# Row-wise squared deviation: two loads from two queues become three loads in one

## The chip, the cores and the metric

The kernel runs on one core of a Trainium2 chip. The metric is the device time of one execution in microseconds (us). Before the change it is 85.28 us, the median of three runs (85.15, 85.28 and 85.28).

## The reference

`x` has 1024 rows of 4096 float32 numbers. From every row its mean is taken away, and the result is squared:

```python
mean = np.mean(x, axis=axis, keepdims=True)      # axis = -1
return ((x - mean) ** 2).astype(np.float32)
```

16.78 MB are read and 16.78 MB are written.

## The kernel before

SBUF has 128 partitions, so each partition handles 8 of the 1024 rows. The kernel splits them into two tiles of four rows per partition (`Q = 4`, `ntiles = 2`). In DRAM the tile index is outermost: tile 0 is the first 512 rows, and partition p holds four neighbouring rows of them, 64 KB in one piece; the next partition's piece begins 64 KB further on. Both tiles have buffers of their own, so no load ever waits for a buffer.

Lines 40 to 48 issue the loads. Row 0 of tile 0 (16 KB per partition, 2 MB in all) is issued from GpSimd (L44), the other three rows of that tile (6 MB) from SP (L45), and the whole of tile 1 (8 MB) from SP (L47). Each of these three transfers has a semaphore of its own, and an instruction that needs a row waits for the transfer that brings it.

Lines 50 to 68 go through the tiles and their rows in order. For each row, VectorE (DVE) sums it with the sign turned (L55, `reduce_sum` with `negate`), multiplies the sum by 1/4096 (L58), and ScalarE (ACT) computes `Square(x + neg_mean)` in place (L59). After every second row (`H = 2`), SP issues a store of these two rows (L68, 4 MB). There are four stores, all in SP's queue.

The statements name what is computed; the order of the instructions on each engine is set by the framework's scheduler. On VectorE it is: reduce 0, mean 0, reduces 1 and 2, mean 1, reduce 3, means 2 and 3, reduces 4 and 5, mean 4, reduce 6, mean 5, reduce 7, means 6 and 7. A mean therefore often comes one reduce later than its own sum. SP issues its instructions in order: both loads, then the four stores, each after waiting for ACT's second row of the pair.

Of the kernel before, what the change touches and what calls it, by code (L numbers as in the profile page):

```python
# [2 lines left out]

os.environ.setdefault("NEURON_RT_ULTRASERVER_MODE", "4")

# [4 lines left out]

F32 = mybir.dt.float32


@with_exitstack
def kernel(
    ctx: ExitStack,
    tc: tile.TileContext,
    x: bass.AP,
    axis: bass.AP,
    out: bass.AP,  # L20
):


    nc = tc.nc

    B, D = x.shape
    P = nc.NUM_PARTITIONS
    Q = 4
    H = 2
    assert B % (P * Q) == 0  # L30
    ntiles = B // (P * Q)
    inv_d = 1.0 / float(D)

    x_t = x.rearrange("(n p q) d -> n p (q d)", p=P, q=Q)
    out_t = out.rearrange("(n p q) d -> n p (q d)", p=P, q=Q)

    io = ctx.enter_context(tc.tile_pool(name="io", bufs=ntiles))
    stats = ctx.enter_context(tc.tile_pool(name="stats", bufs=2 * ntiles * Q))

    tiles = []  # L40
    for i in range(ntiles):
        x_tile = io.tile([P, Q * D], F32)
        if i == 0:
            nc.gpsimd.dma_start(out=x_tile[:, :D], in_=x_t[i][:, :D])  # L44
            nc.sync.dma_start(out=x_tile[:, D:], in_=x_t[i][:, D:])  # L45
        else:
            nc.sync.dma_start(out=x_tile, in_=x_t[i])  # L47
        tiles.append(x_tile)

    for i in range(ntiles):  # L50
        for q in range(Q):
            row = tiles[i][:, q * D:(q + 1) * D]
            neg_sum = stats.tile([P, 1], F32)
            neg_mean = stats.tile([P, 1], F32)
            nc.vector.reduce_sum(  # L55
                out=neg_sum, in_=row, axis=mybir.AxisListType.X, negate=True
            )
            nc.vector.tensor_scalar_mul(out=neg_mean, in0=neg_sum, scalar1=inv_d)  # L58
            nc.scalar.activation(  # L59
                out=row,  # L60
                in_=row,
                func=mybir.ActivationFunctionType.Square,
                bias=neg_mean,
                scale=1.0,
            )
            if q % H == H - 1:
                part = slice((q + 1 - H) * D, (q + 1) * D)
                nc.sync.dma_start(out=out_t[i][:, part], in_=tiles[i][:, part])  # L68


# [1 line left out]
_INS = ['x', 'axis']  # L72
_OUTS = [((1024, 4096), 'float32')]

_NUMBERS = {'axis': -1}


# [26 lines left out]
```

## Time and profile before

| what | value |
|---|---|
| median of the three runs | 85.28 us |
| time of the profiled execution | 85.28 us |
| its span (first to last instruction) | 83.5 us |
| VectorE busy | 35.4 us in 16 instructions; a reduce takes 4.41 us |
| ScalarE busy | 30.7 us in 9 instructions; a row takes 3.70 us |
| bytes over the span | 33.55 MB, mean 402 GB/s |
| load of 6 MB, from issue (0.74) to landing | 21.5 us |
| load of row 0 by GpSimd, from issue (1.22) to landing | 24.0 us |
| load of 8 MB, from issue (1.17) to landing | 41.0 us |
| a store of 4 MB, from issue to landing | 11.2 to 14.7 us |

Transfers are cut into packets, which here are the pieces of one partition: 16, 48 or 64 KB for the loads and 32 KB for the stores. Sixteen DMA engines move them, eight partitions each. In the view by stretches of time, the two DMA columns count a packet wholly in the stretch in which it begins: a stretch shorter than a packet can show a share far above 1 or 0, and only the sums over a round of sixteen packets say how long a packet lasted. In the timeline, an instruction of SP's queue (SPq) is only the issue of a transfer; the transfer itself runs on for many microseconds.

### The profile page before, as it was taken

The page shows a single profiled execution, that of the slowest core. Times are in us where ns is not written, and L with a number is a line of the kernel's source. Part 1 is how long each engine was busy: PE and PEld are TensorE (multiplying, and loading weights), DVE is VectorE, ACT ScalarE, POOL GpSimd, SP SyncE. Part 2 cuts the span into 40 slices and gives each one's busy share as a digit, 9 for nine tenths or more (in the row PEclk, how much of TensorE's full clock was granted, in tenths as well). Part 3 has the DMA queues.
Part 4 walks back from the last instruction along what each step waited for, and adds up shares of the span by engine and source line. Part 5 has one row for each costly group of instructions (what it writes and reads, how often), then busy time and mean ns, then how long its engine had stood idle before and what let it go on. Part 6 is the DMA issues. An engine that isn't in the chain of part 4 may idle for free.

```text
span 83.5 us, 82 instructions
## 1 busy us (share of the span) xinstructions
DVE 35.4 (42%) x16; ACT 30.7 (37%) x9; POOL 0.8 (1%) x5
## 2 busy tenths in 40 slices
DVE  0000000000008999999999999999900000000000
ACT  0000000000006069105969992969799950000000
POOL 4000000000000000000000000000000000000000
DMA  9299999977999659999059599979959996995990
GB/s 306 94 424 439 494 502 502 432 330 330 667 502 471 282 251 502 502 502 502 0 251 502 251 502 502 439 314 502 502 251 502 502 471 282 502 502 251 502 502 0
DMA packets 1008, 33.55 MB, mean 402 GB/s; under 512 B 112, under 2 KB 112, under 8 KB 112
## 3 DMA queue, kind: packets, MB, share of 16 engines
q1 hardware_dynamic: 864, 31.46, 88.2%
q0 software_dynamic: 144, 2.10, 5.9%
HBM read 16.78 MB, written 16.78 MB: 402 GB/s over the span
## 4 chain that ended last, share of the span: by engine, by line
DVE 42%; DMA 29%; ACT 4%; ACTq 4%; issue 1%; POOLq 0%
DVE neg_sum L55 42%; DMA x_tile<-in_x_dram 29%; ACT x_tile L59 4%; ACTq L99 4%; DVE neg_mean L58 1%; POOLq L99 0%; POOLq L85 0%
## 5 line engine op out<-in xcount | busy, mean ns | idle before, releaser
L55 DVE TENSOR_REDUCE neg_sum<-x_tile 128x1 f32<-128x4096 f32 x8 | 35.0, 4410 | 25.3 <-DMA x_tile<-in_x_dram 25.3
L59 ACT ACTIVATE x_tile<-x_tile,neg_mean 128x4096 f32<-128x4096 f32 x8 | 29.4, 3704 | 11.9 <-DVE neg_mean L58 11.9
L59 ACT ACT_TABLE_LOAD x1 | 1.3, 1283 | 25.3 <-DMA x_tile<-in_x_dram 25.3
L58 DVE TENSOR_SCALAR neg_mean<-neg_sum 128x1 f32<-128x1 f32 x8 | 1.1, 148 | 0.0
L44 POOL DMA_DIRECT2D x_tile<-in_x_dram x1 | 0.7, 652 | 0.8 <-PEq L99 0.8
L85 POOL MEMSET const-bfloat16-1.0<- 128x1 bf16 x1 | 0.1, 96 | 0.0
L85 POOL MEMSET const-float32-0.0<- 128x1 f32 x1 | 0.1, 93 | 0.2 <-issue 0.2
L85 POOL MEMSET const-float32-1.0<- 128x1 f32 x1 | 0.1, 93 | 0.0
L85 POOL MEMSET const-uint8-127<- 128x1 uint8 x1 | 0.1, 93 | 0.0
## 6 DMA issues: line engine op xcount, KB each, us to landing
out_dram<-x_tile SPq DMA_DIRECT2D x4, 4096.0 KB, 13.0
x_tile<-in_x_dram SPq DMA_DIRECT2D x1, 6144.0 KB, 21.5
x_tile<-in_x_dram POOLq DMA_DIRECT2D x1, 2048.0 KB, 24.0
x_tile<-in_x_dram SPq DMA_DIRECT2D x1, 41.0
```

What stands on the lines that cost most here:

```text
L44: nc.gpsimd.dma_start(out=x_tile[:, :D], in_=x_t[i][:, :D])
L55: nc.vector.reduce_sum(out=neg_sum, in_=row, axis=mybir.AxisListType.X, negate=True)
L58: nc.vector.tensor_scalar_mul(out=neg_mean, in0=neg_sum, scalar1=inv_d)
L59: nc.scalar.activation(out=row, in_=row, func=mybir.ActivationFunctionType.Square, bias=neg_mean, scale=1.0,)
L85: nc = _bacc.Bacc("TRN2", target_bir_lowering=False, num_devices=1)
L99: with _tile.TileContext(nc) as tc:
```

## The change

The rows are assigned to partitions in another way: partition p now holds the 8 neighbouring rows 8p to 8p + 7 (128 KB in one piece), and the next partition's piece begins 128 KB further on. They are loaded in three transfers of two, four and two rows per partition (4, 8 and 4 MB; packets of 32, 64 and 32 KB), each into a buffer of its own, all issued from SP (L44 of the new file). GpSimd issues no transfer any more. The computation per row is the same, and after every second row a store of two rows (4 MB) is issued from SP (L64), so that there are again four. The diff, without the lines that only lose an indentation:

```diff
-    Q = 4
-    H = 2
-    assert B % (P * Q) == 0
-    ntiles = B // (P * Q)
+    R = B // P
+    LOADS = [2, 4, 2]
+    S = 2
+    assert B == P * R and sum(LOADS) == R
...
-    x_t = x.rearrange("(n p q) d -> n p (q d)", p=P, q=Q)
-    out_t = out.rearrange("(n p q) d -> n p (q d)", p=P, q=Q)
+    x_v = x.rearrange("(p r) d -> p (r d)", p=P)
+    out_v = out.rearrange("(p r) d -> p (r d)", p=P)
...
-    for i in range(ntiles):
-        x_tile = io.tile([P, Q * D], F32)
-        if i == 0:
-            nc.gpsimd.dma_start(out=x_tile[:, :D], in_=x_t[i][:, :D])
-            nc.sync.dma_start(out=x_tile[:, D:], in_=x_t[i][:, D:])
-        else:
-            nc.sync.dma_start(out=x_tile, in_=x_t[i])
-        tiles.append(x_tile)
+    for i, n in enumerate(LOADS):
+        x_tile = io.tile([P, n * D], F32, tag=f"x{i}")
+        nc.sync.dma_start(out=x_tile, in_=x_v[:, r0 * D:(r0 + n) * D])
+        rows += [(x_tile, k) for k in range(n)]
+        r0 += n
...
-            if q % H == H - 1:
-                part = slice((q + 1 - H) * D, (q + 1) * D)
-                nc.sync.dma_start(out=out_t[i][:, part], in_=tiles[i][:, part])
+        if r % S == S - 1:
+            nc.sync.dma_start(
+                out=out_v[:, (r + 1 - S) * D:(r + 1) * D],
+                in_=x_tile[:, (k + 1 - S) * D:(k + 1) * D],
+            )
```

In the changed kernel's order of instructions, VectorE runs reduces 0 and 1, means 0 and 1, reduces 2 and 3, mean 2, reduce 4, mean 3, reduce 5, mean 4, reduce 6, mean 5, reduce 7, means 6 and 7. Reduce 2 waits for the second transfer and reduce 6 for the third. SP issues three loads and then four stores.

More of the change, by code (lines that the diff above doesn't have):

```diff
@@ L27 @@
     P = nc.NUM_PARTITIONS
-    Q = 4
-    H = 2
-    assert B % (P * Q) == 0
-    ntiles = B // (P * Q)
+    R = B // P
+    LOADS = [2, 4, 2]
+    S = 2
+    assert B == P * R and sum(LOADS) == R
     inv_d = 1.0 / float(D)
-    x_t = x.rearrange("(n p q) d -> n p (q d)", p=P, q=Q)
-    out_t = out.rearrange("(n p q) d -> n p (q d)", p=P, q=Q)
-    io = ctx.enter_context(tc.tile_pool(name="io", bufs=ntiles))
-    stats = ctx.enter_context(tc.tile_pool(name="stats", bufs=2 * ntiles * Q))
-    tiles = []
@@ L41 @@
-    for i in range(ntiles):
-        x_tile = io.tile([P, Q * D], F32)
-        if i == 0:
-            nc.gpsimd.dma_start(out=x_tile[:, :D], in_=x_t[i][:, :D])
-            nc.sync.dma_start(out=x_tile[:, D:], in_=x_t[i][:, D:])
-        else:
-            nc.sync.dma_start(out=x_tile, in_=x_t[i])
-        tiles.append(x_tile)
[L50 to L56, printed above, removed]
-            )
[L58 to L65, printed above, removed]
-            if q % H == H - 1:
-                part = slice((q + 1 - H) * D, (q + 1) * D)
-                nc.sync.dma_start(out=out_t[i][:, part], in_=tiles[i][:, part])
+    x_v = x.rearrange("(p r) d -> p (r d)", p=P)
@@ new lines @@
+    out_v = out.rearrange("(p r) d -> p (r d)", p=P)
+    io = ctx.enter_context(tc.tile_pool(name="io", bufs=1))
+    stats = ctx.enter_context(tc.tile_pool(name="stats", bufs=2 * R))
+    rows = []
+    r0 = 0
+    for i, n in enumerate(LOADS):
[3 more added lines that the diff above has]
+        r0 += n
+    for r, (x_tile, k) in enumerate(rows):
+        row = x_tile[:, k * D:(k + 1) * D]
+        neg_sum = stats.tile([P, 1], F32)
+        neg_mean = stats.tile([P, 1], F32)
+        nc.vector.reduce_sum(
+            out=neg_sum, in_=row, axis=mybir.AxisListType.X, negate=True
+        )
+        nc.vector.tensor_scalar_mul(out=neg_mean, in0=neg_sum, scalar1=inv_d)
+        nc.scalar.activation(
+            out=row,
+            in_=row,
+            func=mybir.ActivationFunctionType.Square,
+            bias=neg_mean,
+            scale=1.0,
+        )
+        if r % S == S - 1:
+            nc.sync.dma_start(
+                out=out_v[:, (r + 1 - S) * D:(r + 1) * D],
+                in_=x_tile[:, (k + 1 - S) * D:(k + 1) * D],
+            )
```

## The prediction

> **What bounds the kernel now.** I read the page's DMA digits first, then the queues, then the chain, because the kernel moves 33.55 MB and computes little.
>
> ```profile
> DVE 35.4 (42%) x16; ACT 30.7 (37%) x9; POOL 0.8 (1%) x5
> ...
> DMA  9299999977999659999059599979959996995990
> ...
> q1 hardware_dynamic: 864, 31.46, 88.2%
> q0 software_dynamic: 144, 2.10, 5.9%
> ...
> DVE 42%; DMA 29%; ACT 4%; ACTq 4%; issue 1%; POOLq 0%
> ```
>
> The two queues' packets fill 88.2 + 5.9 = 94.1% of the 16 DMA engines' span: 78.6 of 83.5 us. Only 4.9 us of an average DMA engine is idle. The chain says something else (DVE 42%), and here it misleads: it covers 80% of the span and breaks off at ACT's last row, and the stores that fill the rest are not on it. DVE is busy for 35.4 us and ACT for 30.7 us. So the question is where the 4.9 us lie. The page's 40 slices blur this, because a packet is counted in the slice in which it begins (shares go over 1). I therefore took the stretches view around the places where a stage starts or ends; its last two columns are the DMA share and GB/s.
>
> ```profile
> 1.50:2.00 0.50, 0.00 (x0) 0.00 (x0) 0.38 (x1) 1.00 4.12 1278
> 2.00:2.50 0.50, 0.00 (x0) 0.00 (x0) 0.00 (x0) 1.00 0.60 197
> 2.50:3.00 0.50, 0.00 (x0) 0.00 (x0) 0.00 (x0) 1.00 0.27 98
> 4.00:4.50 0.50, 0.00 (x0) 0.00 (x0) 0.00 (x0) 1.00 2.27 983
> 4.50:5.00 0.50, 0.00 (x0) 0.00 (x0) 0.00 (x0) 1.00 1.36 590
> 38.50:39.00 0.50, 0.50 (x3) 0.38 (x1) 0.00 (x0) 1.00 3.32 1442
> 39.00:39.30 0.30, 0.30 (x1) 0.30 (x1) 0.00 (x0) 1.00 2.02 874
> 39.30:39.40 0.10, 0.10 (x1) 0.10 (x1) 0.00 (x0) 1.00 1.51 655
> 39.40:43.00 3.60, 3.60 (x3) 2.93 (x1) 0.00 (x0) 1.00 0.00 0
> 43.00:43.50 0.50, 0.50 (x2) 0.49 (x1) 0.00 (x0) 1.00 2.44 1049
> 44.00:44.50 0.50, 0.50 (x1) 0.50 (x1) 0.00 (x0) 1.00 1.72 721
> 44.50:45.00 0.50, 0.50 (x1) 0.50 (x1) 0.00 (x0) 1.00 0.78 328
> ```
>
> Two columns give the packets. In 43.0 to 43.5, 1049 GB/s x 0.5 us is 524 KB: 16 packets of 32 KB, one per DMA engine, and 2.44 x 0.5 us says 1.22 us each. In the same way the last round of loads (38.5 to 39.4) is 16 packets of 64 KB at (3.32 x 0.5 + 2.02 x 0.3 + 1.51 x 0.1) = 2.42 us; the second round (4.0 to 5.0) is 16 packets of 48 KB at 1.815 us; the first round takes (4.12 + 0.60 + 0.27) x 0.5 = 2.50 us for the same size, so starting cold costs 0.68 us. All warm sizes run near 27 KB/us per DMA engine: size hardly matters, so the engines' own rate is the limit.
>
> Now the hole. The last round of loads begins at 38.5 to 39.4 and lasts 2.42 us, so loading ends between 40.9 on the first DMA engine and 41.75 on the last (one packet begins alone in 39.3 to 39.4). No store packet begins before 43.0; a finer look puts all 16 between 43.2 and 43.4. Eleven of the 16 last load packets (1442 GB/s x 0.5 us) begin before 39.0, so the average engine ends near 41.3. **The DMA engines stand empty for 1.5 us on the latest and some 1.9 us on average.** The timeline says why:
>
> ```profile
> 25.27 4.42 DVE L55 TENSOR_REDUCE neg_sum<-x_tile 128x1 f32<-128x4096 f32 x1 [25.27 <-DMA x_tile<-in_x_dram]
> ...
> 38.62 3.71 ACT L59 ACTIVATE x_tile<-x_tile,neg_mean 128x4096 f32<-128x4096 f32 x1 [5.00 <-DVE neg_mean L58]
> 42.36 0.35 SPq L68 DMA_DIRECT2D out_dram<-x_tile  x1
> ```
>
> Row 0 is known to have landed only at 25.27, three reduces of 4.41 us follow before the mean of row 1 (issue order: reduce 0, reduces 1 and 2, mean 1), ACT ends row 1 at 42.33, SP issues the first store at 42.36, and its packets begin 0.9 us later. The other idle time is the start (packets from about 1.75) and the close (last store packets begin by 81.1, end by 82.3).
>
> **The change, part by part.**
>
> *Loads.* Bytes are equal. Per DMA engine, now: 8 packets of 48 KB, 8 of 16 KB (GpSimd's, 0.61 us), 8 of 64 KB: 8 x (1.815 + 0.61 + 2.42) + 0.68 = 39.4 us. After: 16 of 32 KB and 8 of 64 KB. A load packet of 32 KB is not in the trace; between twice the 16 KB packet (1.22) and two thirds of the 48 KB one (1.21) it is 1.21, so 16 x 1.21 + 8 x 2.42 + 0.68 = 39.4 us. Difference 0, at most 0.2 either way. The cold excess may be fixed (0.68) or go with size (0.45): at best -0.2.
>
> *GpSimd's issue* (0.65 us) and its queue go; the first packets come from SP's issue at 0.74 in both, so nothing at the start. A gain of 8 x 0.006 = 0.05 us is the upper bound from packets, and no loss is seen since no other instruction waits in POOL. *SP's third load* costs 0.4 us of issue (0.38 and 0.43 now) at 1.6, while the first load's packets run; SP's next work is the store at 29.5. Should SP be held until an earlier load drains, it is 12 us, still free.
>
> *Compute moves forward.* Load 0 (8 rounds) ends at about 1.75 + 0.75 of stagger + 0.68 + 8 x 1.21 = 12.9 on the latest DMA engine and is seen 0.3 to 0.4 later, as now (41.75 against 1.17 + 41.0 = 42.2): 13.2. The new issue order is reduce 0, reduce 1, both means; 13.2 + 2 x 4.4 + 0.1 = 22.1, and ACT's rows 0 and 1 end 2 x 3.7 later: **store 0 is issued at 29.5 instead of 42.36.** It must be there by 40.9: 11.4 us of cover, less 0.9 to the first packet.
>
> *Later stores.* Load 1 ends 8 x 2.42 = 19.4 later, seen at 32.5. The order lags by one: reduces 2, 3, mean 2, reduce 4, mean 3; mean 3 comes at 32.5 + 3 x 4.42 = 45.8, ACT row 3 ends at 49.6, store 1's packets are there at 50.5. Store 0 lasts from 40.9 (41.75 on the latest DMA engine) for 8 x 1.22 = 9.8, to 50.7 (51.5). The margin is 0.2 on the earliest and **1.0 us on the one that sets the end**: the thinnest cover in the plan. Store 2 is issued at about 58.4 for 60.5 (earliest engine), store 3 at 66.6 for 70.2. If load 1 were seen 2 us late, 1.0 us of the gain would go.
>
> *Sum.* The latest DMA engine ends its loads at 41.75 as now, then runs 32 x 1.22 = 39.04 without a hole: 80.8. Now the last packets end at 82.3. That is -1.5 us; landing and close (1.2 us) stay. Span 83.5 - 1.5 = 82.0. The profiled execution took 85.28, 1.78 beyond its span, and 85.28 is also the median: **83.8 us**. An average DMA engine gains 1.9, but the stagger that the first round leaves (0.75) is today swallowed by the hole and will now last to the end; that is why I take 1.5.
>
> *Row pitch.* Each partition's rows now lie 128 KB apart in DRAM instead of 64 KB. All packets of this trace have the old pitch, so the cost is bounded by its best and worst warm rows: stores at the loads' rate (1.21 for 1.22, -0.3 on 32) and every packet slowed like the second round of stores ((1.72 + 0.78) x 0.5 = 1.25 for 1.22: 2.5% of 78.5, +2.0). I take 0: warm packets of four sizes agree to about 1%.
>
> A rule speaks against this. The Trainium skill, "DMA: Bandwidth & Descriptors", section "Latency and other measured facts", lists copies that slow with a large power-of-two distance between partitions' rows: 207 GB/s at 512 KiB against 214 at full rate. If that 3% held here, an estimate from that page adds 2.6 us and makes 86.4; it has no figure at 128 KiB, and no row here shows a second pitch.
>
> Another advises loads and stores on different issuing engines: "Perfetto Trace Analysis", section "DMA Optimizations". By it, store 0 would not stand behind the loads from 29.5 to 41; as the DMA engines are full throughout, the sum stays the same.
>
> **Rivals.**
> 1. *The stagger goes too*, through a shorter first round or less spread at the start: the full 1.9 us is gained, 83.3. For: the stores' starts lie within 0.2 us. Against: the last loads still show the first round's spread 36 us later.
> 2. *Late stores*: store 1 misses its slot and half to all of the hole comes back there, 84.3 to 85.1. For: the margin of 0.2 to 1.0 us. Against: reduces last 4.41 us without scatter.
> 3. *It does not do what it says*: SP cannot queue a store behind unfinished loads, or the packets do not follow without a hole: 85.2. Against: the second load was issued at 1.17 behind 6 MB and followed without a hole.
> 4. *Slower*: the new pitch lengthens packets. It decides from 1.5 / 78.5 = 1.9%; at the bound of 2.5% it gives 85.28 - 1.5 + 2.0 = 85.8. For: it touches all 33.55 MB. Against: warm packets are equally fast at every size, so DRAM seems not to be the limit.
>
> **How the numbers follow.** Forecast 83.8: 0.64. Rival 1: 0.20. Rival 2: 0.08. Rival 3: 0.03. Rival 4: 0.05. The range takes in rival 1 with 0.2 us of packet gains (83.1) and half of rival 2 (84.7). About 0.2% (0.17 us) is what a measurement can tell: faster 0.92, same 0.03, slower 0.05.
>
> **What would show it.** No stretch without packet starts longer than a packet between 1.75 and 81; first store issued near 29.5, the next near 49.6, 58.4 and 66.6; the first reduce near 13.2; last landing near 81.2. A hole near 41 or 51, or warm packets above 1.22 us per 32 KB, would make the prediction wrong.

## The result and the profile after

The changed kernel takes 84.41 us (median of four runs, 84.27 to 84.47), the kernel before beside it 85.22 us (85.04 to 85.28). The ratio is 0.9906, with a 95% interval of 0.9885 to 0.9928: faster by 0.8 us. Forecast were 83.8 us and a gain of 1.5 us, so the sign was right and the time lies in the range, but only about half of the gain came. The profiled execution took 84.35 us with a span of 82.6 us.

From the page of the changed kernel, its queues and its chain:

```profile
DMA  8698990999999099799879998997998999799790
...
q1 hardware_dynamic: 1008, 33.55, 96.1%
...
DMA 37%; DVE 32%; ACT 4%; ACTq 4%; SPq 0%; issue 0%
```

The one queue now fills 96.1% of the DMA engines' span, 79.4 us of 82.6; before, two queues filled 94.1%, 78.6 us. So idle time fell from 4.9 to 3.2 us, but **the same bytes took 0.8 us more packet time**. That second number is what the forecast did not have. The chain again ends with ACT and says nothing about the stores.

The timeline confirms that compute moved forward as planned:

```profile
12.80 8.75 DVE L52 TENSOR_REDUCE neg_sum<-x_tile 128x1 f32<-128x4096 f32 x2 [12.80 <-DMA x_tile<-in_x_dram]
...
28.97 37.23 SPq L64 DMA_DIRECT2D out_dram<-x_tile  x4
```

The first reduce starts at 12.80 (before: 25.27) and store 0 is issued at 28.97 (before: 42.36), long before the loads end. Now the stretches around the places that the prediction spoke of; the last two columns are again DMA share and GB/s, and share times length is the mean duration of a packet if the stretch holds one round of sixteen:

```profile
1.50:2.50 1.00, 0.00 (x0) 0.00 (x0) 0.00 (x0) 1.00 1.78 492
2.50:3.50 1.00, 0.00 (x0) 0.00 (x0) 0.00 (x0) 1.00 0.08 33
37.40:38.00 0.60, 0.60 (x1) 0.00 (x0) 0.00 (x0) 1.00 2.02 874
38.50:39.50 1.00, 1.00 (x1) 0.00 (x0) 0.00 (x0) 1.00 1.72 524
39.50:40.00 0.50, 0.50 (x1) 0.00 (x0) 0.00 (x0) 1.00 0.00 0
40.00:41.00 1.00, 1.00 (x3) 0.02 (x1) 0.00 (x0) 1.00 1.76 524
41.00:41.90 0.90, 0.90 (x1) 0.90 (x1) 0.00 (x0) 1.00 0.00 0
41.90:42.80 0.90, 0.90 (x1) 0.90 (x1) 0.00 (x0) 1.00 1.36 583
79.30:80.30 1.00, 0.00 (x0) 0.00 (x0) 0.00 (x0) 1.00 1.21 524
```

524 GB/s over 1 us is 16 packets of 32 KB. The load round at 37.4 takes 2.02 x 0.6 = 1.21 us, as estimated for a warm load packet of this size. **The last two load rounds take 1.72 and 1.76 us.** The first round of stores (41.9) is back at 1.36 x 0.9 = 1.22, the last (79.3) is at 1.21. There is no hole: 39.5 to 40.0 and 41.0 to 41.9 are empty of starts only because packets last longer. So just ahead of the place where the 1.9 us hole was, two rounds of loads lose 0.51 + 0.55 = 1.06 us on the average DMA engine.

### The profile page after: what moved, and what is told of

It is laid out like the page before. It is cut to its first block, busy times and chain, and to the rows that moved or that the text cites. A ratio compares the mean times of both kernels' runs of the same rounds, so it can differ in the third digit from the quotient of the medians.

```text
span 82.6 us, 83 instructions
## 1 busy us (share of the span) xinstructions
DVE 35.4 (43%) x16; ACT 30.7 (37%) x9; POOL 0.2 (0%) x4
## 3 DMA queue, kind: packets, MB, share of 16 engines
q1 hardware_dynamic: 1008, 33.55, 96.1%
## 4 chain that ended last, share of the span: by engine, by line
DMA 37%; DVE 32%; ACT 4%; ACTq 4%; SPq 0%; issue 0%
DMA x_tile<-in_x_dram 37%; DVE neg_sum L52 32%; ACT x_tile L56 4%; ACTq L98 4%; SPq L44 0%; DVE neg_mean L55 0%
## 5 line engine op out<-in xcount | busy, mean ns | idle before, releaser
L56 ACT ACT_TABLE_LOAD x1 | 1.3, 1283 | 12.8 <-DMA x_tile<-in_x_dram 12.8
```

What stands on the lines that cost most here:

```text
L56: nc.scalar.activation(out=row, in_=row, func=mybir.ActivationFunctionType.Square, bias=neg_mean, scale=1.0,)
```

## The experiments

Three theories were on record before the first run. **Theory A**, the turn: load packets are stretched when stores stand in the queue behind them. **Theory B**: the addresses of the last rows, at the new row pitch, are slow to read. **Theory C**: something that runs between 38 and 43 us disturbs the loads. All times are medians; each ratio is to the kernel before, run on the same chip (85.05 to 85.14 us). All edits but one are made to the changed kernel.

### Store 0 held back by three passes of ACT

`PAD` is 3, and `pad` is a scratch tile of 128 x 4096 ones, so that row 1 is scaled by 1 but waits for the passes:

```diff
+        if r == 1:
+            nc.vector.tensor_scalar(
+                out=pad[:, 0:1], in0=neg_mean, scalar1=0.0, scalar2=1.0,
+                op0=mybir.AluOpType.mult, op1=mybir.AluOpType.add,
+            )
+            for _ in range(PAD):
+                nc.scalar.activation(
+                    out=pad, in_=pad, func=mybir.ActivationFunctionType.Square
+                )
...
-            scale=1.0,
+            scale=pad[:, 0:1] if r == 1 else 1.0,
```

> The changed kernel with three extra passes of ACT over a scratch tile ahead of row 1 (11 us, no other output changes), so that store 0 is issued near 40.0 and its packets come to the DMA engines near 40.9, when at most one load packet is left on each. Theory A: at most the last load packet is stretched, the gain over the changed kernel is 0.5 to 0.9 us: 83.5 to 83.9. Theories B and C: the same two rounds are stretched, 84.4 or more.

Measured: 83.46 us, ratio 0.982 (0.9805 to 0.9834), 1.0 us faster than the changed kernel although ACT does 11 us more, and slightly below the range given. Its stores in the timeline, and its stretches from the same load rounds on:

```profile
39.97 26.20 SPq L77 DMA_DIRECT2D out_dram<-x_tile  x4
...
38.40:39.40 1.00, 1.00 (x1) 1.00 (x1) 0.00 (x0) 1.00 1.21 524
39.40:40.60 1.20, 1.20 (x1) 0.55 (x1) 0.00 (x0) 1.00 1.01 437
40.60:41.10 0.50, 0.50 (x3) 0.14 (x1) 0.00 (x0) 1.00 0.00 0
41.10:42.00 0.90, 0.90 (x1) 0.90 (x1) 0.00 (x0) 1.00 1.36 583
42.00:43.20 1.20, 1.20 (x1) 1.20 (x1) 0.00 (x0) 1.00 1.04 437
```

The last two load rounds take 1.21 us each: same addresses, same time of day, no stretch, because store 0 was issued at 39.97 instead of 28.97. Theory B falls. Theory C falls as far as reduces go (VectorE is busy throughout in both). The second round of stores takes 1.04 x 1.2 = 1.25 us, a small thing that returns below.

### Held back by two passes, and by two and a half

The same edit with `PAD = 2`, and with passes of 4096, 4096 and 2048 columns.

> As the run with three extra passes of ACT, with two: store 0 is issued near 36.3 and is there near 37.2, four us before the loads end. Theory A: the stretch belongs to the last 64 KB (2.4 us), so four us ahead cost as much as twelve: 84.4. If the cost grows with the time that the store stands ready: about a third of it, 83.8.

> As the runs with two and with three extra passes of ACT, with two and a half: store 0 is issued near 38.2 and is there near 39.1, when about two load packets of 32 KB (1.8 to 2.5 us) are left on each DMA engine. Theory A, with the stretch bound to the time that a store stands behind the last 64 KB: between the two, 83.7 to 84.2. If the price is all or nothing: 84.4 or 83.4.

Measured: 84.38 us, ratio 0.9918 (0.9896 to 0.994), with two passes; 83.94 us, ratio 0.9867 (0.985 to 0.9883), with two and a half. With two:

```profile
36.35 29.82 SPq L77 DMA_DIRECT2D out_dram<-x_tile  x4
...
38.50:39.50 1.00, 1.00 (x1) 0.00 (x0) 0.00 (x0) 1.00 2.18 524
40.50:41.50 1.00, 1.00 (x3) 0.54 (x1) 0.00 (x0) 1.00 1.42 524
```

Store 0 is issued at 36.35 and the last two load rounds take 2.18 and 1.42 us: together 1.18 us too much, the full price. The runs with two and a half scatter from 83.92 to 84.34, and the profiled one was the 84.34; its rounds, 1.85 x 1.1 = 2.04 and 0.96 x 1.3 = 1.25 us, show 0.86 us of it. So four us ahead costs as much as twelve, and at about two us ahead (issued at 38.37) the times suggest that the price is paid in some executions and not, or not wholly, in others; only the slowest of the five has a trace.

### Stores with no link to the rows

```diff
-                in_=x_tile[:, (k + 1 - S) * D:(k + 1) * D],
+                in_=con,
```

> The four stores send a constant tile (filled by GpSimd at the start) instead of the squares, so that they wait for no row and stand in SP's queue from the first microseconds on; loads, reduces and squares run as in the changed kernel, but the squares are not stored. Theory A (the turn inside one queue costs by itself): the same two rounds of load packets, the last 64 KB of each DMA engine before the stores, are stretched to about 1.75 us, 84.4. Rival (the cost comes from storing rows that were only just computed, or from what computes at that time): no stretch, 83.4.

Measured: 84.5 us, ratio 0.9928 (0.9911 to 0.9944).

```profile
7.68 1.84 SPq L67 DMA_DIRECT2D out_dram<-con  x4
...
38.40:39.40 1.00, 1.00 (x1) 0.00 (x0) 0.00 (x0) 1.00 1.78 524
40.30:41.20 0.90, 0.90 (x3) 0.21 (x1) 0.00 (x0) 1.00 1.97 583
```

All four stores are issued by 9.5 us, and the last two load rounds still take 1.78 us each (1.78 x 1.0 and 1.97 x 0.9). The stretch starts after 38.4 as in the changed kernel, not when the stores were queued. What is stored, and what computes it, does not matter.

### How the price counts: packets of 64, 16 and 32 KB at the turn

First `LOADS = [2, 2, 4]`, so that the last load packet on each DMA engine is 64 KB; then the last load issued as two of one row, with 16 KB packets:

```diff
-        nc.sync.dma_start(out=x_tile, in_=x_v[:, r0 * D:(r0 + n) * D])
+        step = 1 if i == 2 else n
+        for j in range(0, n, step):
+            nc.sync.dma_start(
+                out=x_tile[:, j * D:(j + step) * D],
+                in_=x_v[:, (r0 + j) * D:(r0 + j + step) * D],
+            )
```

> Loads of two, two and four rows: the packets ahead of the queued stores are 64 KB instead of 32 KB, store 0 stands in the queue from about 29. Theory A, counted in bytes (the last 64 KB of each DMA engine): the one last load packet is stretched by about 1.1 us, from 2.42 to 3.5, 84.4. Counted in packets (the last two): both are stretched by some 45%, 85.5. If the price hangs on small packets: no stretch, 83.3.

> The changed kernel with its last load cut into two loads of one row (packets of 16 KB instead of 32 KB). Theory A, if the turn costs by bytes (the last 64 KB of each DMA engine): the last four packets are stretched, 84.4 as the changed kernel. Theory A, if it costs by packets (the last two): half, 83.9. Theories B and C: 84.4.

Measured: 84.41 us, ratio 0.9924 (0.9909 to 0.9938), and 84.41 us, ratio 0.9927 (0.9913 to 0.9942). Both equal the changed kernel. In the first, one round of 64 KB earlier and the last one (1049 GB/s x 1.0 us and 1311 x 0.8 are 16 packets each):

```profile
36.00:37.00 1.00, 0.00 (x0) 1.00 (x1) 0.00 (x0) 1.00 2.42 1049
38.40:39.20 0.80, 0.00 (x0) 0.25 (x1) 0.00 (x0) 1.00 4.58 1311
```

The last packet takes 4.58 x 0.8 = 3.66 us instead of 2.42: 1.24 us more, on one packet. In the kernel with 16 KB packets, the round begun at 38.6 takes 1.48 x 0.6 = 0.89 us and the next 1.94 x 0.6 = 1.16 us instead of 0.61, the third 1.46 x 0.7 = 1.02, and the fourth is normal again: 1.24 us in all. The price is thus 1.1 to 1.25 us whatever the packets, and it falls on about the last 64 KB of loads of each DMA engine. During it VectorE is idle in the 64 KB kernel and ACT nearly so, which removes theory C for good.

### Smaller stores behind the loads

`S = 1`: eight stores of one row.

> The changed kernel with eight stores of one row (16 KB packets) in place of four of two. Theory A with a price set by the loads' last 64 KB: the same two rounds of load packets are stretched, by 1.1 us in all, 84.4 to 84.6. If the price goes with the size of the store packets that stand behind the loads: half, 83.9.

Measured: 84.73 us, ratio 0.9958 (0.9943 to 0.9972). That is 0.1 us above the range given. The last two load rounds take 1.64 and 0.99 x 2.0 = 1.98 us, 1.2 us too much in all. The price does not fall with the size of the store packets.

### Turning twice, and two queues

The last load issued behind store 0, from four loads of two rows; and, in another kernel, the stores issued from ACT (`nc.scalar.dma_start`):

```diff
+            if r == S - 1:
+                nc.sync.dma_start(out=rows[6][0], in_=x_v[:, 6 * D:8 * D])
```

> Four loads of two rows; the last load is issued behind the first store, so the queue holds load, load, load, store, load, store, store, store and turns from loading to storing twice. Theory A (the turn: the last two load packets ahead of a queued store take 1.75 us instead of 1.21, about 1.07 us per turn): the load packets just ahead of store 0 (near 30) and of store 1 (near 50) are stretched, 0.5 to 1.1 us more in all than the changed kernel, 84.9 to 85.5. Theory B (addresses: the last rows of the new row pitch are slow to read): only the packets of rows 6 and 7 are slow, wherever they stand, 84.4. Theory C (something that computes or reads between 38 and 43 us disturbs the loads): what runs at that time is slow, here stores or loads alike; 84.4.

> The changed kernel with its four stores issued from ACT's queue instead of SP's. Theory A, if the turn belongs to one queue's order: no packet is stretched, the stores start beside the loads at 30, 83.4. Theory A, if a load packet is slow whenever stores stand ready on the same DMA engine: eight or more rounds of load packets from 30 on are stretched by about 0.5 us each, 86 to 89. Theories B and C: 84.4.

Measured: 84.62 us, ratio 0.9955 (0.993 to 0.998), for the two turns: below the range that Theory A gave, so the sum is not two prices. Store 0 was issued at 28.94 and came when about two us of loads were left: the last load round ahead of it is normal (1.54 x 0.8 = 1.23 us). The turn back costs 0.27 us (the last store round ahead of the load, at 39.6: 1.48 instead of 1.21). The second turn to stores, with store 1 queued for ten us, costs 0.05 + 0.62 us (1.26 in the round at 48.4, then 1.41 x 1.3 = 1.83):

```profile
49.70:51.00 1.30, 0.00 (x0) 0.00 (x0) 0.00 (x0) 1.00 1.41 403
```

A turn is cheap where the store comes late and dear where it has stood there, but 0.67 is less than 1.06, and the runs do not say why.

With the stores on ACT's queue: 84.81 us, ratio 0.9965 (0.9949 to 0.998). Both numbers that Theory A gave were wrong. From its stretches:

```profile
28.60:29.60 1.00, 0.00 (x0) 0.26 (x1) 0.00 (x0) 1.00 2.57 1049
31.00:32.50 1.50, 0.00 (x0) 0.00 (x0) 0.00 (x0) 1.00 1.34 350
33.00:34.20 1.20, 1.20 (x1) 0.00 (x0) 0.00 (x0) 1.00 1.11 437
34.40:35.40 1.00, 1.00 (x1) 0.00 (x0) 0.00 (x0) 1.00 1.23 524
...
60.90:62.00 1.10, 0.45 (x3) 0.75 (x1) 0.00 (x0) 1.00 0.01 0
```

Store 0 is issued at 28.89, and from then on loads and stores share the DMA engines: the third load, of 4 MB, is seen to have landed only at 52.35. The rounds in which the stores begin are stretched: 2.57 for 2.42, 1.34 x 1.5 = 2.01, 1.33, 1.23, together 0.15 + 0.80 + 0.12 + 0.02 = 1.1 us. After that the mixed packets run at 1.21 us until the loads are done. So it is not the order inside one queue, and not mixing as such: **the price is paid once, where stores begin among loads that are still under way.** The hole of 0.6 us near 61 is another matter: the third store stands on ACT behind row 6, which waits for the late third load, so it was issued only at 61.26.

### Loads of four and four, in both row pitches

`LOADS = [4, 4]` at the new pitch; and the kernel before with one edit, at the old pitch:

```diff
-        if i == 0:
-            nc.gpsimd.dma_start(out=x_tile[:, :D], in_=x_t[i][:, :D])
-            nc.sync.dma_start(out=x_tile[:, D:], in_=x_t[i][:, D:])
-        else:
-            nc.sync.dma_start(out=x_tile, in_=x_t[i])
+        nc.sync.dma_start(out=x_tile, in_=x_t[i])
```

> The changed kernel with two loads of four rows instead of three of two, four and two: the loads' split as before, but all in SP's queue. Store 0 is issued near 38.7 and is there near 39.6, one to two us before the loads end. Theory A, if the cost grows with how long the store stands ready inside the last 2.4 us: a part of the stretch, 83.6 to 84.1. Theory A with a fixed price per turn: 84.4.

> The kernel before with one edit: its first tile comes in one load of four rows from SP's queue, nothing from GpSimd's; tiles and row pitch (64 KB) stay as before. If the new row pitch costs or brings nothing, it equals the run with two loads of four rows at the new pitch: 83.2. If the new pitch brought part of that gain: 83.5 or more; if it cost something: below 83.0.

Measured: 83.19 us, ratio 0.978 (0.976 to 0.9799), and 83.25 us, ratio 0.9787 (0.9773 to 0.9802). The first lies below both numbers on record, the second was expected. They agree, so **the row pitch is worth nothing measurable** (64 against 128 KB), and both beat the kernel before, by 1.8 to 1.95 us, and the changed kernel, by 1.2 us. In both the first reduce starts at 22.5 or 22.6 us instead of 25.27, since nothing waits for GpSimd's load of row 0 any more, and store 0 is issued at 39.49 and 39.58 instead of 42.36. At the new pitch:

```profile
38.40:39.20 0.80, 0.80 (x1) 0.80 (x1) 0.00 (x0) 1.00 3.04 1311
39.20:41.00 1.80, 1.04 (x3) 1.12 (x2) 0.00 (x0) 1.00 0.00 0
41.00:42.00 1.00, 0.13 (x1) 1.00 (x1) 0.00 (x0) 1.00 1.22 524
42.00:43.20 1.20, 1.20 (x1) 1.20 (x1) 0.00 (x0) 1.00 1.01 437
```

The last load round takes 3.04 x 0.8 = 2.43 us, unstretched, the stores follow it without a hole (starts at 39.2 at the latest, plus 2.43, reaches into the store round at 41.0) and run at 1.01 x 1.2 = 1.21 us. Issued 39.5, so there at about 40.4 by the 0.9 us seen before: half a us to 1.2 us ahead of the end of the loads. This lucky spot has neither hole nor stretch. My estimate of its issue time, 38.7, missed that mean 1 comes after reduce 2 in this order.

### Paced by a landing

The last load cut so that its last 1536 columns come by themselves, and a one-column operation of GpSimd on store 0's tile that waits for the piece before:

```diff
+        if r == S - 1:
+            last = rows[-1][0]
+            nc.gpsimd.tensor_scalar(
+                out=x_tile[:, 0:1], in0=x_tile[:, 0:1],
+                scalar1=last[:, 0:1], scalar2=last[:, 0:1],
+                op0=mybir.AluOpType.add, op1=mybir.AluOpType.subtract,
+            )
```

> The changed kernel, with its last load cut so that a last piece of 1536 numbers per partition (1.8 us) comes by itself, and with store 0 held back until the piece before it has landed (a one-column operation of GpSimd on the store's tile waits for it). No work is added on VectorE or ACT. Store 0 should reach the DMA engines as the loads end. Theory A: 83.3 to 83.8, faster than both kernels; the rival that the stretch is bound to addresses or to the time of day: 84.4.

Measured: 83.6 us, ratio 0.9821 (0.98 to 0.9841). The operation runs at 40.25 for 0.37 us, store 0 is issued at 40.65 and no load packet is stretched, but the stores come a little late: they start only after the first DMA engines have run out of loads, most of them after 41.3, and run at 1.75 x 0.7 = 1.22 and 2.50 x 0.5 = 1.25 us. It ties the time of the store to the loads instead of to the compute, at 0.4 us over the lucky spot.

## Why the prediction was half right

**What held.** The hole was there, it came from the late store 0, and it is gone. The DMA engines and nothing else set the end. Compute moved as worked out, each event 0.4 to 0.7 us earlier than put: first reduce 12.80 (13.2), stores issued at 28.97, 49.10, 57.88 and 65.86 (29.5, 49.6, 58.4, 66.6). No later store was late. Warm load packets of 32 KB take 1.21 us as estimated, and the cold excess of the first round is 0.65 us ((1.78 + 0.08) x 1.0 = 1.86 against 1.21), so nearly fixed. The row pitch costs nothing: 64 and 128 KB give 83.25 and 83.19 us, and the estimate of 86.4 us that was drawn from the Trainium skill's "DMA: Bandwidth & Descriptors" (section "Latency and other measured facts") does not hold at 128 KB. The other advice that the prediction cited, separate issuing engines for loads and stores (the Trainium skill, "Perfetto Trace Analysis", section "DMA Optimizations"), cost 0.4 us here against one queue (84.81 to 84.41), in a run in which one store came late.

**The step that failed** is the first sentence of the sum: "The latest DMA engine ends its loads at 41.75 as now." It cost the last 64 KB of loads at their old duration, since in the trace of before nothing ever stood behind them: the stores came after an empty stretch. With a store waiting there, the last loads take 1.06 us longer on average in the profiled execution, and the latest DMA engine turns to its first store at 42.7. The runs that hold the store back until those packets have nearly gone through (83.46, 83.6, 83.19 us) get this back.

**The rest of the sum**, for the latest DMA engine: -1.5 us for the hole; -0.3 because the first round left less stagger than before, a part of rival 1 (on every DMA engine the second load packet begins by 4.0, and 7 x 1.21 + 8 x 2.42 + 8 x 1.21 us later it is 41.5 instead of 41.75); +1.2 for the turn (42.7 instead of 41.5; the average engine lost 1.06); and -0.3 because store packets take 1.21 instead of 1.22 us, 32 of them. Together -0.9 us; the profiled executions differ by 0.93 (85.28 to 84.35). Without the turn it would have been -2.1; the loads of four and four measure -1.8 to -1.95 by their medians, and -2.1 by their profiled executions (83.15 and 83.22). So two small errors in the other direction hid part of the big one, and the forecast of 1.5 was too low for what the idea can give and too high for this form of it. That 84.41 still lies in the range is luck: its upper end, 84.7, was put there for late stores, which did not come, and nothing in the range stood for slow packets at the end of the loads. One of the signs of being wrong that the prediction named did appear: warm packets above 1.22 us per 32 KB.

**The rivals.** Rival 1 (stagger) happened in part. Rivals 2 and 3 did not: stores followed loads without a hole. Rival 4 had the right symptom, longer packets, with the wrong cause and place: not all packets by 2.5%, but 64 KB per DMA engine by 45%.

**What stays open.** Why the price is near 1.1 us, why 64 KB, and why the second turn to stores in one kernel cost only 0.67. The Trainium skill, "DMA: Bandwidth & Descriptors", section "Two DMAs through the same engine are not ordered", says that an engine's read and write sides are separate queues and that descriptors are pipelined; stores being read ahead while loads are still being written would fit that picture, but no run here shows the two sides apart.

## What to carry to other kernels

A hole between the last load and the first store can be closed by queueing the store earlier, but in these runs a store that stood ready more than about two us before the loads ended made the last 64 KB of loads per DMA engine cost 1.1 us more, so earlier was not better: the best time came with the store there 0.5 to 1.2 us ahead. When a step puts a new neighbour behind a transfer, its old duration is a bound and not a price, and the range should hold a term for the new neighbour. And starting compute as early as possible was not the aim here: the changed kernel starts its first reduce at 12.8 us and takes 84.41 us, while the kernel before with one edit, all loads from one queue in two equal parts, starts it at 22.6 and takes 83.25, 1.8 us less than without the edit.

## What the runs showed of the hardware that was not expected

- Storing that begins among loads under way costs about 1.1 us once (1.06 to 1.25 us in seven kernels; 0.86 and 0.67 in two cases), with 16, 32 or 64 KB load packets, 16 or 32 KB store packets, one queue or two. Where both went on side by side afterwards (stores on ACT's queue), they shared the DMA engines at 1.21 us per 32 KB packet.
- Stores that follow the loads without a hole run at 1.21 us per packet; after a hole they run at 1.22, with a second round of 1.25 (kernel before, the run with three passes of ACT and the paced one). Over 32 packets that is 0.2 to 0.3 us, about the difference between 83.46 and 83.19; the runs do not say why.
